# A hybrid decoder layer on eight cores: shift folded into biases, convolution weights built on the core, shuffles in one DMA, and a new order of loads

## The chip, the cores and the metric

The kernel runs on the 8 cores of one Trainium2 chip. Each core computes one batch element, and the cores don't talk to each other. The metric is device time in microseconds (us) of the slowest core. "Granted clock" is the share of full speed that TensorE was given, 1.00 being all of it. The profile views are of the slowest core of one execution; the trace holds all eight. The program lets TensorE write its results into eight banks of 128x512 fp32, in a memory called PSUM, and has VectorE or ScalarE copy ("evict") each result out before it uses the bank again; one such copy took ScalarE 0.60 us in the kernel before (`ev<-ps`, mean of 136).

## The reference, cut to what matters

```python
# x (8, 2048, 1024) fp32, c (8, 1024); one layer
mod = silu(c) @ w_ada + b_ada                       # adaLN: 6 pieces of 1024
sh1, sc1, gt1, sh2, sc2, gt2 = split(mod, 6)
h = rmsnorm(x, g_pre_mix) * (1 + sc1) + sh1
gb, gc, v, a, g = split(h @ w_in, 5)                # 5 x 512 columns
y_short = gb * (causal_dwconv(gc * v, w_short) + b_short)       # 3 taps
u = causal_dwconv(a * sigmoid(g), w_cfm_dw) + b_cfm_dw          # 31 taps
y_cfm = silu(layernorm(u, g_cfm_ln, b_cfm_ln))
y = per_head_rmsnorm(concat(y_short, y_cfm)) * beta_mix
x = x + gt1 * rmsnorm(y @ w_out, g_post_mix)
h = rmsnorm(x, g_pre_ffn) * (1 + sc2) + sh2
x = x + gt2 * rmsnorm(swiglu(h, w_gate_up, w_down), g_post_ffn) # hidden 2816
```

## The kernel before

The kernel brings its own scheduler: the code below is a list of operations with their reads, writes and estimated cost, and the scheduler orders them on each engine. Weights are fp32 in DRAM and bf16 in SBUF; they come by DMAs that POOL issues (the software queue, 53.48 MB in the page), and the other transfers go through SP's hardware queue (48.32 MB). The sequence is cut in four quarters of 512 positions, quarter q holding the positions 4t+q. For the 31-tap convolution the four quarters stand side by side in the partitions, 4 x 32 channels, so that a group of 32 channels takes 9 matmuls. Bringing the projections into that layout, and the result back out of it, is a "shuffle", a DMA from SBUF to SBUF.

The start, with one quarter's gate projections. All four adaLN pieces of the first sub-layer come ahead of the gate weights, and a shuffled tile leaves as four DMAs:

```python
for half in range(2):
    ada_cols(half, "sc", 0, half, (4, 5))
for half in range(2):
    ada_cols(2 + half, "sh", 0, half, (4, 5))
wag = [wload(wag_d[i], 4096, "wag%d" % i) for i in range(2)]
prenorm1(0)
for q in range(4):
    if q < 3:
        prenorm1(q + 1, after=[loads["wada2" if q == 0 else "wag1"]])
    for j in range(4):
        ...                                          # gate and value projections
        act(th, gb.v(), AF.Tanh, scale=0.5, name="tanh")
        dve("scalar_tensor_tensor", ..., name="glu") # (th + 1) * value -> sv
        for c in range(4):
            dv = up.v(g * URow + HALO, g * URow + HALO + CH, 32 * q, 32 * q + 32)
            prs.append((dv.ap, sv.v(p0=32 * c, p1=32 * c + 32)))
        dma("sp", prs, [sv.v()], wv, 0.7, "ushuf")   # four DMAs
```

The convolution (16 groups, weights loaded for two groups at a time), then LayerNorm over channels in one block, then the head norm:

```python
for g in range(NG):
    if g % 2 == 0:
        cw = wload(cw_d[g // 2], 2 * NTAP * 128, "cw%d" % (g // 2))
    ...                                              # 9 matmuls, two evictions, statistics
for g in range(NG):
    dve(ln_sub); dve(ln_mul); act(silu)
for h in range(0, 8, 2):
    ...                                              # head norm, y shuffle: four DMAs a tile
```

Then come the C and v projections, and the output stage: `short(q)` is the 3-tap branch of a quarter, `outproj(q)` its output projection with the residual, and `ada_rows` makes the broadcast row gt1 * g_post_mix, for which it takes a small row from DRAM into one of the two `ys` buffers:

```python
short(0); ada_rows(4, 0, 0, B05); ada_rows(5, 0, 1, B05)
short(1); outproj(0, (2, 4))
short(2); outproj(1, (2, 4))
short(3); outproj(2, (4,)); outproj(3, (4,))
...                                                  # FFN: gate/up, silu, down, residual
```

Four `slot` buffers hold all the weights but `wo` and `wdn`. The two `wo` buffers lie in the memory of `u1`, the convolution's result, so the output projection's weights can only be loaded once the head norm has read it. The four `xc` tiles (x for the residual) lie where the LayerNorm rows were.

Of the kernel before, what the change touches and what calls it, by code (L numbers as in the profile page):

```python
# [36 lines left out]
NV = V_WSH + 12  # L37

# [53 lines left out]
class Prog:  # L92
# [111 lines left out]
    def schedule(self):  # L204
# [53 lines left out]
        while len(seq) < n:  # L258
# [51 lines left out]
            if o.dma is not None:  # L310
                s = max(free[e] + 1000.0, dma_free)
                dma_free = s + o.dma
                o.done = dma_free + 1200.0
            else:
                o.done = free[e] + o.lat
# [149 lines left out]
def build_program():  # L465
# [5 lines left out]
    wag_d = nc.dram_tensor("wag", [2, 128, 4096], F32, kind="ExternalInput").ap()  # L471
    cw_d = nc.dram_tensor("cw", [8, 128, 2 * NTAP * 128], F32, kind="ExternalInput").ap()
# [10 lines left out]
    with es:  # L483
# [35 lines left out]
        assert wdn[1].end <= end_stg  # L519
        xa_s = sb_space("xa", 8, D, F32, at=yT.off)  # L520
        xc_off = cur[0]
        xc_s = sb_space("xc", 4, D, F32)
        lnb = [buf("ln%d" % i, 512, F32, at=xc_off + 2048 * (5 + i)) for i in range(3)]
        xn_s = sb_space("xn", 4, D, BF16)
        ev_s = sb_space("ev", 4, 512, F32)
        ys_s = sb_space("ys", 2, 512, F32)
# [11 lines left out]
        small = buf("small", 192, F32)  # L538
        SM_EPS, SM_EXP, SM_SH, SM_GS, SM_T, SM_SSQ, SM_RS = 0, 1, 2, 18, 34, 50, 114
# [28 lines left out]
        def mm(out, lhsT, rhs, start, stop, n=512, reads=(), name="", **kw):  # L568
            return P.op("pe", lambda e: e.matmul(out.ap, lhsT=lhsT.ap, rhs=rhs.ap, start=start, stop=stop),  # L569
                        reads=[lhsT, rhs] + list(reads), writes=[out], cost=max(n / 2.4 + 2.8, 60.0), lat=280.0,  # L570
                        name=name, **kw)

        def act(out, in_, func, n=512, reads=(), writes=(), name="", bias=None, scale=1.0, accum=None, npt=0, **kw):
# [5 lines left out]
            tb = "silu" if func in (AF.Silu, AF.Tanh) else "exp" if func in (AF.Ln, AF.Exp) else None  # L579
# [14 lines left out]
        def dma(eng, pairs, reads, writes, us, name="", **kw):  # L594
            def fn(e):
                return [e.dma_start(out=val(o_), in_=val(i_)) for o_, i_ in pairs]  # L596
            o = P.op(eng, fn, reads=reads, writes=writes, cost=(1000.0 if eng == "pool" else 70.0) * len(pairs), dma=us * 1000.0,
                     name=name, **kw)
            o.ndma = len(pairs)
            return o  # L600


        loads = {}

        def wload(src, n, name):
            s = Tile(slot_s)
            v = s.v(0, n)
            loads[name] = dma("pool", [(v, src)], [], [v], 128 * n * 4 / 350e3, name=name)
            return s
# [8 lines left out]
        dve("memset", [], [blk32.v()], 250, "c4", ap=blk32.t[:, :], constant=0.0)  # L618
        dve("memset", [], [blk64.v()], 250, "c5", ap=blk64.t[:, :], constant=0.0)

        dve("memset", [], [ones_ln.v()], 250, "c6", ap=ones_ln.t[:, :], constant=0.0)
        for p in range(4):
            a, b = 32 * p, 32 * p + 32
            dve("memset", [], [ones_ln.v(0, 128, a, b)], 180, "c7", ap=ones_ln.t[a:b, a:b], constant=1.0 / 512.0)
            dve("memset", [], [blk32.v(0, 128, a, b)], 180, "c7", ap=blk32.t[a:b, a:b], constant=1.0 / 64.0)
# [12 lines left out]
        act(ct, View(vc(V_C, 8), [K_V]), AF.Silu, n=8, name="csilu")  # L638
# [12 lines left out]
        def ada_cols(piece, kind, l, half, banks):  # L651
# [15 lines left out]
            else:  # L667
                bcol = V_BADA + 16 * l + 8 + 4 * half
                dve("tensor_tensor", [b.v(), K_V], [("sh", l, half)], 80, "ada3", out=sm(SM_SH + c, 4), in0=b.v(0, 4),
                    in1=vc(bcol, 4), op=ALU.add)  # L670

        def ada_rows(piece, l, half, banks):
# [6 lines left out]
            tv = Tile(ys_s).v()  # L679
# [22 lines left out]

        def to_hT(xns, q, l, last, banks):

            for quarter in range(4):
# [9 lines left out]
                for kk in range(2):  # L715
# [4 lines left out]
                    if quarter % 2 == 0:  # L720
# [9 lines left out]
        def prenorm1(q, after=()):  # L730
            xns = []
            last = None
            for b in range(4):
                i = 4 * q + b
                xt = Tile(xa_s).v()
                dma("sp", [(xt, xq[q, b])], [], [xt], 1.5, "xload", after=after)
# [6 lines left out]
        xns = []  # L743
        for half in range(2):
            ada_cols(half, "sc", 0, half, (4, 5))
        for half in range(2):
            ada_cols(2 + half, "sh", 0, half, (4, 5))
        wag = [wload(wag_d[i], 4096, "wag%d" % i) for i in range(2)]
        prenorm1(0)
# [5 lines left out]
        B05 = (0, 1, 2, 3, 4, 5)  # L755
        for q in range(4):
            if q < 3:
                prenorm1(q + 1, after=[loads["wada2" if q == 0 else "wag1"]])
            for j in range(4):
                w, o = wag[j // 2], (j % 2) * 2048  # L760
                gb, ab = bank('mm', *B05), bank('mm', *B05)
                proj(gb, w, o, q, "pg", also=[ab])
                proj(ab, w, o + 1024, q, "pa")
                th = Tile(ev_s).v()
                act(th, gb.v(), AF.Tanh, scale=0.5, name="tanh")
                sv = Tile(stg_s)
                dve("scalar_tensor_tensor", [th, ab.v()], [sv.v()], 750, "glu", out=sv.v(), in0=th, scalar=1.0, in1=ab.v(),
                    op0=ALU.add, op1=ALU.mult)
                prs, wv = [], []
                for c in range(4):  # L770
                    g = 4 * j + c
                    dv = up.v(g * URow + HALO, g * URow + HALO + CH, 32 * q, 32 * q + 32)
                    prs.append((dv.ap, sv.v(p0=32 * c, p1=32 * c + 32)))
                    wv.append(dv)
                dma("sp", prs, [sv.v()], wv, 0.7, "ushuf")
# [5 lines left out]
        for g in range(NG):  # L781
            if g % 2 == 0:
                cw = wload(cw_d[g // 2], 2 * NTAP * 128, "cw%d" % (g // 2))
            b = bank('mm', *B05)
            for s in range(NTAP):
                o = ((g % 2) * NTAP + s) * 128
# [3 lines left out]
            act(uv, b.v(), AF.Identity, reads=[K_V], bias=vc(V_BCF + g), scale=0.5, npt=1, name="cv_ev")  # L790
            s1 = Tile(sq_s).v()
            act(s1, b.v(), AF.Square, reads=[K_V], bias=vc(V_BCF + g), scale=0.5, npt=1, name="cv_sq")
# [12 lines left out]
        P.shift = LN_SHIFT  # L805
        last_silu = None
        for g in range(NG):
# [3 lines left out]
            last_silu = act(uv, uv, AF.Silu, reads=[K_V], bias=vc(V_BLN + g), scale=vc(V_GLN + g), npt=2, name="silu")  # L811
        for h in range(0, 8, 2):
# [8 lines left out]
            rr = Tile(rr_s, line="hdrr")  # L821
            act(rr.v(), st.v(), AF.Ln, n=1024, reads=[("eps",)], bias=sm(SM_EPS), npt=1, name="hd_ln", order=[last_silu])
            act(rr.v(), rr.v(), AF.Exp, n=1024, scale=-0.5, name="hd_exp")
            for h2 in range(2):
                for gg in range(2):
# [6 lines left out]
                    prs, wv = [], []  # L832
                    j, c = g // 4, g % 4
                    for p in range(4):
                        o = (4 + j) * S + p * CH
                        dv = yT.v(o, o + CH, 32 * c, 32 * c + 32)
                        prs.append((dv.ap, sv.v(p0=32 * p, p1=32 * p + 32)))
                        wv.append(dv)
                    dma("sp", prs, [sv.v()], wv, 0.7, "yshuf")
        P.shift = 0.0  # L840
# [6 lines left out]
        dma("sp", [(gtg[0].t[:, :], r_d[0:1, :].to_broadcast([128, D]))], [], [gtg[0].v()], 1.6, "rowb", after=[loads["cw5"]])  # L847
        wcv = [None, None]
        for j in range(4):
            if j % 2 == 0:  # L850
                wcv[j // 2] = wload(wcv_d[j // 2], 4096, "wcv%d" % (j // 2))
            w, o = wcv[j // 2], (j % 2) * 2048
            cb = cvb[j]
            for q in range(4):
# [4 lines left out]
                act(cs, b1.v(), AF.Copy, name="c_ev")  # L859
                ov = cb.v(q * URow + HALO, q * URow + HALO + CH)  # L860
                dve("tensor_tensor", [cs, b2.v()], [ov], 690, "cv", out=ov, in0=cs, in1=b2.v(), op=ALU.mult)
# [7 lines left out]
        wb = wload(wb_d, 4096, "wb")  # L869
        last_exp = [None]  # L870

        def short(q):
            for jp in range(2):
                st = pair('sh', 6)
                yss = [Tile(ys_s), Tile(ys_s)]
                for j2 in range(2):
                    j = 2 * jp + j2
                    b3, b4 = bank('mm', *B05), bank('mm', *B05)
                    proj(b3, wb, j * 1024, q, "pb", also=[b4])
                    bs = Tile(ev_s).v()  # L880
                    act(bs, b3.v(), AF.Copy, name="b_ev")
# [11 lines left out]
                rr = Tile(rr_s)  # L893
                act(rr.v(), st.v(), AF.Ln, n=1024, reads=[("eps",)], bias=sm(SM_EPS), npt=1, name="sh_ln", order=[last_silu])
# [46 lines left out]
        short(2)  # L941
        outproj(1, (2, 4))
        short(3)
# [5 lines left out]
        npc = [0]  # L949
        for half in range(2):  # L950
            for pc in range(11):
                n_ = npc[0]
                npc[0] += 1
                early = half == 0 and pc < EARLY
                w = wload(wgu_d[pc], 4096, "wgu%d" % pc)
                for jj in range(2):
                    j = 2 * pc + jj
                    for s in range(2):
                        q = 2 * half + s
                        gb, ub = (bank('gu', 0, 1, 2, 3), bank('gu', 0, 1, 2, 3)) if early else (bank('gu', *range(8)), bank('gu', *range(8)))  # L960
                        for u, b in enumerate((gb, ub)):
                            for k in range(8):
                                o = ((jj * 2 + u) * 8 + k) * 128
                                mm(b.v(), w.v(o, o + 128), hv(k, q), k == 0, k == 7, name="gu", also=[ub] if u == 0 and k == 0 else ())
                        sl = Tile(ev_s).v()
                        act(sl, gb.v(), AF.Silu, name="fsilu", order=[last_exp[0]])
                        av = actT.v(j * 1024 + s * 512, j * 1024 + s * 512 + 512)
# [115 lines left out]
```

## Time and profile before

| | before |
|---|---|
| time, median of 4 runs | 849.3 us (846.68 to 849.69) |
| profiled span, slowest core | 847.7 us |
| TensorE busy | 749.6 us, 88% |

The first line of the profile's page gives each engine's busy time, its share of the span and its instructions. For the kernel before:

```profile
PE 749.6 (88%) x3737; PEld 349.5 (41%) x3808; DVE 273.6 (32%) x408; ACT 256.1 (30%) x409; POOL 83.0 (10%) x185
```

TensorE (PE) is far above the rest.

### The profile page before, as it was taken

The page shows a single profiled execution, that of the slowest core. Times are in us where ns is not written, and L with a number is a line of the kernel's source. Part 1 is how long each engine was busy: PE and PEld are TensorE (multiplying, and loading weights), DVE is VectorE, ACT ScalarE, POOL GpSimd, SP SyncE. Part 2 cuts the span into 40 slices and gives each one's busy share as a digit, 9 for nine tenths or more (in the row PEclk, how much of TensorE's full clock was granted, in tenths as well). Part 3 has the DMA queues.
Part 4 walks back from the last instruction along what each step waited for, and adds up shares of the span by engine and source line. Part 5 has one row for each costly group of instructions (what it writes and reads, how often), then busy time and mean ns, then how long its engine had stood idle before and what let it go on. Part 6 is the DMA issues. An engine that isn't in the chain of part 4 may idle for free.

```text
span 847.7 us, 10294 instructions; the slowest of 8 cores (834.2 to 847.7 us)
## 1 busy us (share of the span) xinstructions
PE 749.6 (88%) x3737; PEld 349.5 (41%) x3808; DVE 273.6 (32%) x408; ACT 256.1 (30%) x409; POOL 83.0 (10%) x185
## 2 busy tenths in 40 slices
PE   0177999967859798899999999999999999999996
PEld 0134544433324344444444444444444444444442
DVE  3114521482223466645421132122222211111222
ACT  1135525694205466734331111111111111111111
POOL 2103100000000112221200000000100000000100
PEclk9998999979979899999999999999999999999999
DMA  8998149959676334996899676233344544001221
GB/s 153 187 203 243 34 79 160 165 96 198 134 141 124 100 115 110 189 254 163 164 164 198 110 134 114 51 124 115 110 99 68 82 75 76 0 1 49 101 75 75
DMA packets 26066, 102.46 MB, mean 121 GB/s; under 512 B 4256, under 2 KB 8480, under 8 KB 20512
## 3 DMA queue, kind: packets, MB, share of 16 engines
q0 software_dynamic: 7344, 53.48, 38.0%
q1 hardware_dynamic: 18672, 48.32, 18.6%
q8 instruction: 31, 0.51, 0.2%
q14 instruction: 19, 0.16, 0.1%
HBM read 134.29 MB, written 16.78 MB: 178 GB/s over the span
## 4 chain that ended last, share of the span: by engine, by line
PE 74%; DMA 12%; DVE 4%; issue 4%; ACT 3%; SPq 2%; POOL 1%; POOLq 0%; DVEq 0%; ACTq 0%
PE ps L569 72%; DMA yT<-stg 5%; DMA xa<-x 4%; DMA slot<-wada 4%; SPq L596 2%; ACT junk L581 1%; DVE u L585 1%; PE ps L712 1%; ACT rr L581 1%; DVE xc L585 1%; POOL small L589 1%; DVE ps L585 1%; ACT L581 0%; DVE yT L585 0%; DVE ys L585 0%
## 5 line engine op out<-in xcount | busy, mean ns | idle before, releaser
L569 PE MATMUL ps<-hT,slot 128*128 128x512 bf16 x2002 | 460.1, 385 | 23.4 <-DVE small L585 8.7
L569 PEld LDWEIGHTS ps<-hT,slot 128*128 128x128 bf16 x2048 | 201.2, 99 | 267.0 <-issue 37.8
L581 ACT ACTIVATE ev<-ps 128x512 f32<-128x512 f32 x136 | 81.0, 595 | 301.2 <-PE ps L569 292.6
L569 PE MATMUL ps<-wdn,actT 128*128 128x512 bf16 x689 | 151.3, 379 | 0.7
L585 DVE TENSOR_TENSOR actT<-ev,ps 128x512 bf16<-128x512 f32 x88 | 60.4, 686 | 204.1 <-PE ps L569 196.2
L569 PEld LDWEIGHTS ps<-wdn,actT 128*128 128x128 bf16 x704 | 68.9, 98 | 83.0
L585 DVE SCALAR_TENSOR_TENSOR ps<-ps,small,gtg 128x1024 f32<-128x1024 f32 x32 | 41.4, 1293 | 138.2 <-POOL small L589 138.2
L581 ACT ACTIVATE junk<-ps 128x1024 bf16<-128x1024 f32 x32 | 32.7, 1022 | 166.7 <-PE ps L569 158.1
L569 PE MATMUL ps<-wo,yT 128*128 128x512 bf16 x252 | 58.6, 384 | 4.2 <-DVE xc L585 3.6
L589 POOL TENSOR_SCALAR small<-small 128x1 f32<-128x1 f32 x64 | 16.2, 254 | 370.3 <-ACT junk L581 369.7
L712 PE MATMUL ps<-ident,xn 128*128 128x128 bf16 x256 | 21.4, 247 | 28.9 <-DVE xn L585 27.3
L585 DVE TENSOR_TENSOR xc<-ps,xc 128x1024 f32<-128x1024 f32 x32 | 39.1, 1223 | 4.0 <-DVE ps L585 4.0
L569 PEld LDWEIGHTS ps<-wo,yT 128*128 128x128 bf16 x256 | 25.1, 99 | 36.1 <-issue 8.2
L589 POOL TENSOR_TENSOR small<-small 128x1 f32<-128x1 f32 x64 | 37.5, 585 | 9.5 <-POOL small L589 0.6
L569 PE MATMUL ps<-up,slot 128*128 128x512 bf16 x141 | 33.4, 379 | 0.2
L712 PEld LDWEIGHTS ps<-ident,xn 128*128 128x128 bf16 x256 | 19.1, 112 | 33.8 <-issue 32.2
L596 POOL DMA_DIRECT2D slot<-wgu x22 | 12.3, 558 | 198.0 <-PE ps L569 197.8
L581 ACT ACTIVATE hT<-ps,small 128x512 bf16<-128x512 bf16 x32 | 23.2, 775 | 20.7 <-PE ps L712 11.8
L569 PE MATMUL ps<-cact,slot 128*128 128x1 bf16 x256 | 7.9, 165 | 22.1 <-DMA slot<-wada 16.9
L581 ACT ACTIVATE junk<-xa 128x1024 bf16<-128x1024 f32 x16 | 16.8, 1053 | 30.6 <-DMA xa<-x 30.0
L585 DVE SCALAR_TENSOR_TENSOR stg<-ev,ps 128x512 bf16<-128x512 f32 x16 | 11.0, 688 | 37.3 <-PE ps L569 31.3
L585 DVE SCALAR_TENSOR_TENSOR stg<-u,vt,rr 128x512 bf16<-128x512 f32 x16 | 11.7, 750 | 32.6 <-DMA yT<-stg 30.5
(62 smaller groups left out, 328.1 us busy)
## 6 DMA issues: line engine op xcount, KB each, us to landing
slot<-wgu POOLq DMA_DIRECT2D x22, 1024.0 KB, 10.2
slot<-wada POOLq DMA_DIRECT2D x12, 1024.0 KB, 16.6
xa<-x SPq DMA_DIRECT2D x16, 512.0 KB, 12.7
xc<-x SPq DMA_DIRECT2D x16, 512.0 KB, 5.5
x1s<-xc SPq DMA_DIRECT2D x16, 512.0 KB, 6.0
xc<-x1s SPq DMA_DIRECT2D x16, 512.0 KB, 3.9
out<-xc SPq DMA_DIRECT2D x16, 512.0 KB, 2.6
slot<-cw POOLq DMA_DIRECT2D x8, 576.0 KB, 7.9
```

What stands on the lines that cost most here:

```text
L569: return P.op("pe", lambda e: e.matmul(out.ap, lhsT=lhsT.ap, rhs=rhs.ap, start=start, stop=stop), reads=[lhsT, rhs] + list(reads), writes= ...
L581: return P.op("act", lambda e: e.activation(out=out.ap, in_=in_.ap, **a), reads=[in_] + list(reads), writes=[out] + list(writes), cost=c, ...
L585: return P.op("dve", lambda e: getattr(e, meth)(**{k: val(v) for k, v in kw.items()}), reads=reads, writes=writes, cost=cost, lat=80.0, na ...
L589: return P.op("pool", lambda e: getattr(e, meth)(*a, **kw), reads=reads, writes=writes, cost=cost, lat=80.0, name=name)
L596: return [e.dma_start(out=val(o_), in_=val(i_)) for o_, i_ in pairs]
L712: P.op("pe", lambda e, ov=ov, iv=iv: e.transpose(out=ov.ap, in_=iv.ap, identity=ident.t[:, :]), reads=[iv, ident.v()], writes=[ov], cost=6 ...
```

## The change

The intent is to start TensorE sooner, to take bytes out of the DMA queues where they hold it up, and to take small work out of its way. There are five parts.

1. The adaLN shift is not added to h but becomes biases after the projections (`w.T @ shift`, one-column matmuls). Two of the four adaLN pieces are enough for the first projection. Quarter 0's projections wait raw in SBUF for their biases. The first loads of x move from SP's queue into POOL's, in line with the weights, and the gate weights come in four loads with buffers of their own.
2. Convolution weights are multiplied out of a small table (0.29 MB in DRAM) on VectorE, instead of eight loads of 1.18 MB.
3. A new channel layout makes each shuffled tile one DMA and not four.
4. LayerNorm and head norm are spread behind the C/v projections; the weights of this stage wait for the last input shuffle (HELD); the first four residual x loads go behind the last y shuffle.
5. In the output stage: `short(3)` ahead of `outproj(1)`, more banks, four `ys` buffers, one own buffer for the row, and gate/up products of quarter 0 first.

```diff
-        for half in range(2):
-            ada_cols(2 + half, "sh", 0, half, (4, 5))
-        wag = [wload(wag_d[i], 4096, "wag%d" % i) for i in range(2)]
-        prenorm1(0)
+        wag = [wload(wag_d[i], 2048, "wag%d" % i, wag_s) for i in range(4)]
+        xts.append(xload(1))
+        prenorm1(0, xts[0])
 ...
+                if q == 0:
+                    act(rg, gb.v(), AF.Copy, name="raw")
+                    dve("tensor_copy", [ab.v()], [ra], 690, "raw", out=ra, in_=ab.v())
+                    raws.append((j, q, rg, ra))
 ...
+                    ada_cols(2 + half, "sh", 0, half, (6, 7))
+                bias([(wag[i // 2], (i % 2) * 1024) for i in range(8)], (6, 7), 0)
 ...
-                cw = wload(cw_d[g // 2], 2 * NTAP * 128, "cw%d" % (g // 2))
+            dve("tensor_tensor", [wv.v(), dlt.v()], [cw.v()], 1300, "cwm", out=ov,
+                in0=dlt.t[:, :].unsqueeze(1).unsqueeze(3).to_broadcast([128, NTAP, 32, NPH]),
+                in1=w3.unsqueeze(2).to_broadcast([128, NTAP, 32, NPH]), op=ALU.mult)
 ...
-                    dma("sp", prs, [sv.v()], wv, 0.7, "yshuf")
+                    ysl.append(dma("sp", [(dv, sv.v())], [sv.v()], [View(None, wk)], SHUF, "yshuf"))
+        behind = {i: [lambda g=g: ln(g) for g in range(2 * i, 2 * i + 2)] for i in range(8)}
+        for i in range(4):
+            behind[8 + 2 * i] = [lambda h=h: head_norm(h) for h in (2 * i,)]
 ...
-        ys_s = sb_space("ys", 2, 512, F32)
+        row_s = sb_space("row", 1, 512, F32)
+        ys_s = sb_space("ys", 4, 512, F32, at=u1.off)
 ...
-            tv = Tile(ys_s).v()
+            tv = Tile(row_s).v()
 ...
         short(2)
+        short(3)
         outproj(1, (2, 4))
-        short(3)
 ...
+        ys = [o for o in P.q["sp"] if o.name == 'yshuf'][-1]
+        xs = [o for o in P.q["sp"] if o.name == 'xload2'][:4]
 ...
+                L.remove(o)
+            i = L.index(ys) + 1
 ...
+            L[i:i] = xs
```

## The prediction

> **What bounds the kernel now.** I read the page first: TensorE is busy 88% of the span, so it is the bound, and a gain can only come from its idle or slowly clocked time. The second view, busy time by stretch cut where TensorE changes its task, says where that time lies (columns: stretch, its length, busy time and count of each engine, granted clock, DMA share, GB/s).
>
> ```profile
> 0.00:50.78 50.78, 7.24 (x160) 7.21 (x162) 11.32 (x52) 8.98 (x14) 8.84 (x22) 1.00 0.95 175
> 50.78:71.54 20.76, 15.92 (x62) 6.63 (x63) 5.70 (x8) 6.64 (x12) 3.51 (x8) 0.94 1.01 238
> 71.54:120.52 48.98, 48.54 (x284) 25.45 (x290) 19.09 (x31) 24.16 (x40) 8.81 (x17) 0.96 0.35 92
> 120.52:158.12 37.60, 37.39 (x171) 17.03 (x174) 7.70 (x20) 19.16 (x31) 4.23 (x8) 1.00 0.89 153
> 158.12:253.66 95.54, 70.31 (x397) 31.79 (x402) 42.61 (x73) 44.26 (x64) 4.22 (x8) 0.86 0.79 146
> 253.66:356.36 102.70, 89.50 (x429) 40.87 (x436) 57.11 (x70) 60.56 (x92) 17.30 (x39) 0.95 0.53 125
> 356.36:839.69 483.33, 480.69 (x2239) 220.56 (x2283) 127.59 (x154) 91.20 (x157) 35.29 (x81) 1.00 0.48 106
> 839.69:847.70 8.01, 0.00 (x0) 0.00 (x0) 2.52 (x2) 1.11 (x2) 0.79 (x2) 0.75 0.16 65
> ```
>
> The stretches are: loading before the first projection; gate projections (two rows); the 31-tap convolution; the C/v projections with LayerNorm and head norm behind them; the short branch and output projection; the FFN; the tail. The FFN and the convolution are full. Idle: 43.5 us at the start, 5.3 in the gate projections, 25.2 in the C/v stage, 13.2 in the output stage, 8.0 in the tail.
>
> The chain that ended last names what the idle parts wait for (start, duration, what):
>
> ```profile
> 3.15 31.52 DMA slot<-wada
> ...
> 36.56 31.65 DMA xa<-x
> ...
> 174.66 1.35 DVE u L585 x3
> ...
> 189.91 14.49 DMA yT<-stg
> ...
> 209.86 11.58 DMA yT<-stg
> ...
> 229.55 13.20 DMA yT<-stg
> ```
>
> So: weights and x at the start; then, in the C/v stage, the LayerNorm run on VectorE (32 operations, 161.4 to 182.6 us, with evictions of projections queued behind them: the first three come at 182.48), then three shuffles. The waits of that stage, TensorE's own and VectorE's on the shuffle (total us, times, longest):
>
> ```profile
> DVE stg L585 <- DMA yT<-stg: 30.5, 5, 12.0
> ...
> PE ps L569 <- DVE small L585: 8.7, 1, 8.7
> PE ps L569 <- ACT sq L581: 7.7, 4, 5.0
> PE ps L569 <- DVE cvb L585: 7.4, 3, 4.0
> PE ps L569 <- ACT ev L581: 1.2, 2, 1.0
> ```
>
> VectorE stands on a staging buffer that a shuffle has not emptied, so it evicts no projection, and TensorE runs out of PSUM banks.
>
> [...] in the FFN the chain repeats every 10.79 us for 50 matmuls (49 recorded, some records are missing), and 14 matmuls after a stall took 4.91 us[...]. [...] a shuffle piece lands in 1.8 us on idle DMAs and in 8 to 14.7 us while the software queue streams weights. [...] by 83.25 us some 23.4 MB of fp32 source had landed, 289 GB/s counted from 2.3 us. [...]
>
> **Start and gate projections.** Before, x (four tiles, 2.1 MB), four adaLN pieces (8.4 MB fp32) and the first gate weights (2.1 MB) precede the first projection at 50.78 us. The change folds the shift into biases applied after the projections, so only two adaLN pieces are needed first, and cuts the gate weights into 1 MB loads. What must land falls from 12.6 to 2.1 + 4.2 + 1.05 = 7.3 MB. At 289 GB/s that is 25 us plus 2.3; the slower rate of the first 42 us (10.5 MB in 40 us, 262 GB/s) gives 30. First projection: about 30, 20 earlier. That gain does not last whole. The next tiles queue behind in one software queue: gate weights, x of quarter 1 (12.6 MB landed at 46 us), the two shift pieces (61), x of quarters 2 and 3 (69, 76). In the new order of instructions TensorE stands in line for both shift pieces inside quarter 1, then computes biases, and the first quarter's raw gates hold staging buffers until then. Following the order: quarter 1 starts near 51, its last projections near 75 (they need banks that the late gates release), quarter 2 near 80, and two quarters of 13.8 us with transposes of 2 put the convolution at 107 to 110; at 310 GB/s it would be 103. I take 107 for 120.5: **-13.5 us**.
>
> **Convolution.** The eight weight loads (1.18 MB each) go; VectorE builds the diagonal weights from a small table. 16 operations of 1152 elements[...]; four are made ahead. [...] Hidden: **0**.
>
> **C/v stage.** LayerNorm is now spread two groups behind each of the first eight projections, one head norm behind every second of the last eight; each staged tile leaves in one DMA instead of four (64 issues of 0.59 us become 16); x for the residual no longer queues ahead of the shuffles; weights for this stage are loaded during the convolution. Work: 272 matmuls x 0.216 = 58.8, 128 one-column ones in 4.0 (32 took 0.99 us), 64 new bias columns 2.0: 64.8 us against 95.5 taken. What remains lost: in the first half VectorE has 32 x 0.60 us (28 LayerNorm operations took 16.95 us back to back in the timeline) and 8 x 0.75, 25 us beside 29.6 of TensorE, so only the latency of the statistics shows (5 us from the last convolution to the first subtraction with its scale, less what spare banks cover): 3 us. In the second half three 2.1 MB weights still stream when the first four tiles shuffle, and four staging buffers remain, so one or two waits of 8 us stand, partly covered by spare banks: 6 us. Stage 74: **-21.5 us**.
>
> **Output stage.** Short branch 3 before output projection 1, more banks and buffers for it, and gate/up products of quarter 0 first, so they can fill holes without quarter 1. Idle is 13.2 us, slow clock (5% of 89.5) about 4. VectorE and ScalarE stay half busy, and their chains (evict, square, ln, exp, multiply) remain: I take off 8. **-8 us**.
>
> **Sum.** The 160 bias columns (5 us) are counted in the stages. 849.3 - 13.5 - 21.5 - 8 = 806.3; the size of the C/v gain leans to the low side, since the held loads look placed against just that wait, so I say **805 us**.
>
> **Rivals.** (1) The start's gain is given back: DMA share is 1.01 until about 83 us, and x of quarter 3 cannot land before 76, so the convolution starts at 115 and the total is 815 to 820. For it: the two in-order waits on shift pieces. Against: 2.1 MB less must land by then, and nothing waits for convolution weights. (2) The shuffles stay the wait of the C/v stage: same bytes, same staging buffers, weights still streaming; the stage keeps 20 lost us and the total is 820 to 825. For it: the 8 to 14 us landings above. Against: the residual's x, which stood ahead in the same queue for the first of the three waits, is gone. (3) VectorE becomes the bound in the convolution[...]; 813. (4) The stages close fully: C/v dense, output stage dense, 785 to 790.
>
> **Range and chances.** Start gain 5 to 18, C/v 10 to 28, output 2 to 13, not moving together: 788 to 825. Slower would need gains to vanish in three independent places. Faster by over 2% (below 832) 0.95, same 0.045, slower 0.005.
>
> **What would show it.** First wide matmul near 30 us; convolution weights' first use at 103 to 110; its stretch still 38 us with VectorE about 30 busy; C/v stage 70 to 80 us with clock above 0.93; VectorE's wait on the shuffle well under 30.5; FFN and tail unchanged. Wrong if the convolution starts after 115, if the C/v stage is over 85, or if the FFN gets a wait.

Three figures given there without a source can be found in the trace of the kernel before: 0.216 us a matmul is the FFN's 10.79 us for 50; 0.75 us is what VectorE took for 512 columns of `ys<-ps,vt,ev` (750 ns, median); and 310 GB/s is near what the text's own numbers give for the time after 42 us (23.4 less 10.5 MB in 41.25 us, 313 GB/s). The DMA share that rival 1 puts at 1.01 until about 83 us is 1.01 from 50.78 to 71.54 us and 0.81 from there to 83.25.

## The result, and the profile after

The changed kernel takes 818.56 us, median of 10 runs (fast ones 816.45 to 819.71), against 849.01 for the kernel before, median of 16 in the same rounds. Executions in which one die ran at a lower clock are left out of the means. The ratio of the fast runs is 0.9641, with a 95% interval of 0.9629 to 0.9653: faster by over 2%. (Ratios here divide the mean time of one kernel's fast runs by that of the other's of the same rounds, so they are not quite the ratio of the medians quoted.) The profiled span went from 847.7 to 818.2 us.

The page's first line of the changed kernel: VectorE has 24.5 us more work (the built weights are 21.5 of it), and TensorE's busy time hardly moved, so the gain is idle time of TensorE.

```profile
PE 752.8 (92%) x3969; PEld 351.1 (43%) x3969; DVE 298.1 (36%) x429; ACT 261.2 (32%) x413; POOL 92.6 (11%) x196
```

Busy time by stretch of the changed kernel, cut at the same changes of task as before (the same columns: stretch, length, PE, PEld, DVE, ACT, POOL, granted clock, DMA share, GB/s):

```profile
0.00:29.96 29.96, 5.81 (x97) 5.26 (x98) 11.23 (x47) 8.62 (x14) 16.17 (x35) 1.00 0.93 180
29.96:54.93 24.97, 18.06 (x81) 8.33 (x81) 5.78 (x8) 7.59 (x14) 6.31 (x12) 0.93 1.01 212
54.93:113.21 58.28, 52.57 (x400) 27.48 (x401) 26.74 (x42) 25.98 (x43) 10.04 (x16) 0.94 0.44 121
113.21:151.62 38.41, 38.41 (x207) 17.82 (x206) 23.26 (x33) 19.96 (x32) 2.22 (x4) 1.00 0.69 113
151.62:226.96 75.34, 67.89 (x481) 32.77 (x478) 44.10 (x75) 45.30 (x63) 3.69 (x7) 0.95 0.58 102
226.96:320.00 93.04, 82.11 (x387) 36.48 (x386) 47.12 (x61) 55.32 (x80) 13.14 (x29) 0.96 0.72 168
320.00:810.80 490.80, 487.99 (x2328) 222.97 (x2326) 137.36 (x163) 97.96 (x169) 40.26 (x92) 1.00 0.47 106
810.80:818.20 7.40, 0.00 (x0) 0.00 (x0) 2.52 (x2) 0.48 (x2) 0.79 (x2) 0.63 0.18 71
```

| step | before | after | moved by | forecast |
|---|---|---|---|---|
| first wide matmul | 50.78 | 29.96 | -20.8 | about 30 |
| convolution starts | 120.52 | 113.21 | -7.3 | -13.5 |
| convolution | 37.60 | 38.41 | +0.8 | 0 |
| C/v stage | 95.54 | 75.34 | -20.2 | -21.5 |
| output stage and FFN together | 586.03 | 583.84 | -2.2 | -8 |
| tail | 8.01 | 7.40 | -0.6 | 0 |

The output stage and the FFN have to be read together, because the number of gate/up steps that run ahead went from six to four, and with it the line between the two. The rows below the first make 29.5 us, the difference of the two spans.

The chain that ended last (start, duration, what) goes, as before, through x at the start and through shuffles; a row of 256 KB is new in it:

```profile
20.02 49.70 DMA xa<-x
...
193.25 18.97 DMA yT<-stg
...
214.60 17.50 PE ps L581 x99
...
237.65 0.69 DVE gtg L597
...
238.50 0.70 DVE gtg L597
239.26 25.27 DMA row<-rows
```

And the waits (total us, times, longest), TensorE's first, then VectorE's on transfers:

```profile
PE ps L746 <- DVE xn L597: 24.6, 3, 14.8
PE ps L581 <- DVE small L597: 7.4, 1, 7.4
PE ps L581 <- DVE ys L597: 6.2, 1, 6.2
```

```profile
DVE stg L597 <- DMA yT<-stg: 15.5, 3, 8.4
...
DVE gtg L597 <- DMA row<-rows: 4.7, 2, 4.4
```

The first line of the waits is the start (14.8 us until the first x is normalised) and two later tiles of x. The second is the C/v stage: its whole idle time is this one wait at 214 us, and behind it stands the shuffle issued at 193.25, which needed 19 us. (`small` is only the tiny operation that VectorE did last; VectorE had been standing on the staging buffer.) The third is new: at 267.6 us TensorE waits 6.2 us for the short branch's `ys`, and the chain shows why. The second row load was issued at 239.26 us, the moment VectorE had used the first row, and took 25 us to land.

These are the waits of core 7, the slowest. In the same execution the C/v wait is 5.2 to 7.4 us on four cores (spans 813.5 to 818.2 us) and at most 1.9 us on the other four (806.1 to 809.3 us): it takes the slow cores, and the metric is the slowest one. The wait for `ys` is on all eight cores, 1.1 to 9.6 us.

### The profile page after: what moved, and what is told of

Same layout as the page of the kernel before. It is cut to its first block, busy times and chain, and to the rows that moved or that the text cites. A ratio compares the mean times of both kernels' runs of the same rounds, so it can differ in the third digit from the quotient of the medians.

```text
span 818.2 us, 10617 instructions; the slowest of 8 cores (806.1 to 818.2 us)
## 1 busy us (share of the span) xinstructions
PE 752.8 (92%) x3969; PEld 351.1 (43%) x3969; DVE 298.1 (36%) x429; ACT 261.2 (32%) x413; POOL 92.6 (11%) x196
## 4 chain that ended last, share of the span: by engine, by line
PE 74%; DMA 15%; DVE 3%; ACT 3%; issue 2%; POOL 1%; POOLq 0%; DVEq 0%; ACTq 0%; SPq 0%
PE ps L581 73%; DMA xa<-x 7%; DMA row<-rows 3%; DMA yT<-stg 2%; DMA slot<-wgu 2%; ACT junk L593 2%; PE ps L746 1%; DVE xc L597 1%; DVE ps L597 1%; POOL small L601 1%; DMA up<-stg 1%; ACT ev L593 0%; DVE stg L597 0%; ACT rs L593 0%; POOL xa L608 0%
## 5 line engine op out<-in xcount | busy, mean ns | idle before, releaser
L581 PE MATMUL ps<-hT,slot 128*128 128x512 bf16 x1792 | 398.8, 381 | 16.0 <-DVE small L597 7.4
L581 PEld LDWEIGHTS ps<-hT,slot 128*128 128x128 bf16 x1792 | 174.9, 98 | 228.0 <-issue 22.5
L593 ACT ACTIVATE ev<-ps 128x512 f32<-128x512 f32 x88 | 52.4, 597 | 217.0 <-PE ps L581 217.0
L581 PE MATMUL ps<-hT,wag 128*128 128x512 bf16 x256 | 61.8, 401 | 2.7 <-DMA wag<-wag 2.0
L601 POOL TENSOR_SCALAR small<-small 128x1 f32<-128x1 f32 x64 | 18.0, 282 | 358.8 <-ACT junk L593 358.3
L593 ACT ACTIVATE ev<-ps,small 128x512 f32<-128x512 f32 x44 | 29.8, 680 | 39.0 <-PE ps L581 35.1
L581 PEld LDWEIGHTS ps<-hT,wag 128*128 128x128 bf16 x256 | 25.5, 102 | 33.9 <-issue 8.6
L581 PE MATMUL ps<-up,cw 128*128 128x512 bf16 x144 | 33.6, 379 | 0.0
L597 DVE TENSOR_TENSOR cw<-dlt,wv 128x1152 bf16<-128x1152 bf16 x16 | 21.5, 1357 | 9.9 <-PE ps L581 7.7
```

The source lines that it names most:

```text
L581: return P.op("pe", lambda e: e.matmul(out.ap, lhsT=lhsT.ap, rhs=rhs.ap, start=start, stop=stop), reads=[lhsT, rhs] + list(reads), writes= ...
L593: return P.op("act", lambda e: e.activation(out=out.ap, in_=in_.ap, **a), reads=[in_] + list(reads), writes=[out] + list(writes), cost=c, ...
L597: return P.op("dve", lambda e: getattr(e, meth)(**{k: val(v) for k, v in kw.items()}), reads=reads, writes=writes, cost=cost, lat=80.0, na ...
L601: return P.op("pool", lambda e: getattr(e, meth)(*a, **kw), reads=reads, writes=writes, cost=cost, lat=80.0, name=name)
```

## The experiments

Twelve kernels ran, four at a time on one chip, each beside the kernel before. Where not said otherwise an edit is made to the changed kernel. On the chip of the first four, the kernel before was unsteady (849.17 to 863.82 us, median 860.55), so I read those four against the changed kernel's 818.56 us, or the 820.18 of the later control, and do not use their ratios. The unedited changed kernel did not run on that chip; on the two chips where it did, it differs by 1.6 us.

### The first four: take out one part at a time

**LayerNorm and head norm in one block again** (`ln_block`):

```diff
-        behind = {i: [lambda g=g: ln(g) ...] for i in range(8)}
-        for i in range(4):
-            behind[8 + 2 * i] = [lambda h=h: head_norm(h) for h in (2 * i,)]
+        behind = {}
+        for g in range(NG):
+            ln(g)
+        for h in range(0, 8, 2):
+            head_norm(h)
```

> The changed kernel with one part undone: all LayerNorm and head norm work stands in one block before the C/v projections again. Theory (the block on VectorE was the larger cause of the 20 us that the C/v stage gained): TensorE idles again behind it, the stage grows from 75.3 us by 10 to 15, the total goes from 818.6 to 828 to 834. Rival (the shuffles were the cause, the spread is incidental): the stage grows by under 4, total at most 822. A third way: the shuffles start some 10 us earlier this way and meet fewer weight loads, so part of the loss is paid back and the total is 822 to 828.

It took 817.25 us (816.24 to 818.06): not slower. My theory of this part fell. TensorE's waits show what was exchanged:

```profile
PE ps L581 <- ACT sq L593: 5.7, 3, 4.0
...
PE ps L581 <- DVE cvb L597: 3.1, 2, 2.3
```

The block costs several short waits, the longest 4.0 us. In return the 7.4 and the 6.2 us are gone: the y shuffles are issued from 179 us on rather than 192, the residual x at 214 rather than 227 and lands by 245 rather than 262. In this kernel, spreading the norms delays what comes after them by about as much as it saves.

**Each shuffle as four DMAs again** (`shuf4`), in the new layout, so a piece covers 8 destination partitions by 4 rows:

```diff
-            ush.append(dma("sp", [(dv, sv.v())], ...
+            ush.append(dma("sp", [(dv[8 * c:8 * c + 8], sv.v(p0=32 * c, p1=32 * c + 32)) for c in range(4)], ...
```

(and the same for the y shuffles)

> The changed kernel with every shuffle issued as four DMAs of 32 rows again, same bytes and same layout. Theory (the number of issues was not what cost; the rows wait behind the weight loads in the DMA engines): within 2 us of 818.6. Rival (the queue's 64 issues of 0.59 us were the wait): the C/v stage grows by 5 to 10 us, total 824 to 829.

829.68 us (828.83 to 831.22), 9.5 to 11 slower: my theory fell. But these pieces are cut differently from those of the kernel before, which left open whether the count or the cut costs. `shuf4b` below settles it.

**The residual x not moved** (`xres_early`): the block that moves the four loads is deleted.

> The changed kernel without the step that moves the first four residual x loads behind the last head shuffle; they are issued before the shuffles, during the convolution. Theory (moving them shifted a wait from one stage to another, and they would have landed long before the shuffles start): the C/v stage unchanged within 2 us, the output stage loses most of the 6.2 us stall near 262 to 267 us, since x and the row behind it no longer land at 259 to 265; total 812 to 818. Rival (they stand in front of the shuffles as in the kernel before): C/v stage longer by 5 or more, total 820 to 824.

825.94 us, the median of the three fast runs (825.42 to 829.49), 6 to 7 slower; here too my theory fell, and the rival held, a little beyond its range. TensorE's and VectorE's waits:

```profile
PE ps L581 <- DVE small L597: 27.4, 2, 16.2
```

```profile
DVE stg L597 <- DMA yT<-stg: 35.9, 3, 24.5
```

The `xc` buffers come free only at 180 us, so the loads are issued just ahead of the shuffles. The first four shuffles then take 27 us each.

**The shift pieces ahead of the gate weights** (`shift_first`), to take the early start away and leave the rest:

```diff
+        for half in range(2):
+            ada_cols(2 + half, "sh", 0, half, (4, 5))
         wag = [wload(wag_d[i], 2048, "wag%d" % i, wag_s) for i in range(4)]
```

(and the later call is removed)

> The changed kernel with the two shift pieces loaded before the gate weights, as in the kernel before; biases are still applied after the projections. Theory (the convolution's start is set by when x of quarters 2 and 3 has landed, and the same bytes must land by then in both orders): the first wide matmul comes at about 44 us instead of 30, the convolution starts at 110 to 117 instead of 113.2, total 816 to 822. Rival (the early start is worth its 14 us): convolution at 125, total 829 to 833.

822.54 us (822.15 to 823.0), 2 to 4 slower: the theory's direction, just outside of its ranges. The first wide matmul comes at 44.24 us, 14.3 later, the convolution at 119.39, only 6.2 later, and the end 2 to 4 later. That is the early start's exchange rate: less than half of it reaches the convolution, and under a third the end. The edit undoes 14.3 of the 20.8 us; the rest, with x in POOL's queue and smaller gate loads, was not taken apart.

### The second four: what is left, and the control

**Control** (`after_ctl`), the changed kernel unedited:

> Control: the changed kernel itself once more, so that the variants of this batch have their parent on the same chip. 816 to 820 us if this chip is like the one of the first measurement.

820.18 us (816.99 to 824.78), ratio 0.9658 (0.962 to 0.9696). Slightly more spread than in the first measurement.

**adaLN columns 6 to 9 ahead of the C/v projections** (`ada_early`). In the changed kernel the four weight slots were full from 148 to 167 us and the DMAs idle (share 0.01); the last weights then streamed beside the shuffles.

```diff
-            if j == 0:
-                ada_cols(6, "sc", 1, 0, B05)
-            elif j == 1:
-                ada_cols(7, ...); ada_cols(8, ...)
-            elif j == 2:
-                ada_cols(9, "sh", 1, 1, B05)
+            # in front of the first C/v projection, after wcv0 is asked for:
+            ada_cols(6, ...); ada_cols(7, ...); ada_cols(8, ...); ada_cols(9, ...)
```

> adaLN columns 6 to 9 are computed before the C/v projections instead of inside them, so the four weight slots come free some 25 us earlier and the last 2.1 MB weights stream in the hole of the DMA between 148 and 167 us and not beside the y shuffles. Theory (the y shuffles are slow because weights stream beside them): shuffles land in 3 to 8 us instead of 18 to 19, the 7.45 us wait of TensorE at 214 us falls below 3, time 5 to 8 us less, 810 to 814. Rival (the shuffles are slow by their own issue and count): they stay at 15 us or more, the wait stays, time 817 to 820. Third way: wada6 to 9 land late enough that TensorE waits for them in front of the C/v projections: slower by up to 5 us.

816.12 us, the median of the three fast runs (815.33 to 818.62), ratio 0.9613 (0.9588 to 0.9638): 0.45% of 849 us, some 3.8 us, less than the control. The two intervals overlap, so the gain in time is not clear of the scatter, and it falls short of the 5 to 8 us of the theory; what the edit did to the waits is clear. DMA issues of the page (what, queue, operation, count, size, median us from issue to landing), first of the changed kernel, then of this one:

```profile
yT<-stg SPq DMA_DIRECT2D x16, 128.0 KB, 8.8
```

```profile
yT<-stg SPq DMA_DIRECT2D x16, 128.0 KB, 3.4
```

The first twelve shuffles now land in 2.9 to 3.4 us (2.9 to 3.7 over all eight cores), and the 7.4 us wait is gone (at most 0.3 us on any core): the shuffles were slow because weights streamed beside them. The last four are not better off, 10 to 27 us, because the weights of the output projection and of the FFN stream from 213 us on. TensorE now waits there, 3.2 us for a shuffle and 5.7 us (at 263.5 us) for VectorE's residual adds. VectorE itself waits for no staging buffer any more, but for the row:

```profile
DVE gtg L597 <- DMA row<-rows: 13.6, 1, 13.6
```

The row lands at 258.6 us, and the second one, in the same buffer, at 262.8. So what took the place of the removed wait is the subject of the next run.

**A second row buffer** (`row2`):

```diff
-        row_s = sb_space("row", 1, 512, F32)
+        row_s = sb_space("row", 2, 512, F32)
```

> A second buffer for the broadcast row of the quarter, so that the second row load need not wait until VectorE has used the first. Theory (the new 6.2 us wait of TensorE at 267.6 us hangs on the single row buffer, through which the issues that follow stand in line): the wait falls to under 2 us, time 3 to 6 us less. Rival (the loads land late, 259 to 264 us, because 2.1 MB weights for the output stage stream ahead of them on all engines): the wait stays at 5 to 6 us, time unchanged within 1.5 us.

814.21 us (813.09 to 816.31), ratio 0.9587 (0.9565 to 0.9609): 0.71%, some 6 us, less than the control, from one digit. The two rows are issued together (237.4 and 238.9 us) and land at 262.9 and 263.6. In the control the second is issued at 265.9 and lands at 269.3. TensorE's waits, first of the control, then of this run:

```profile
PE ps L581 <- DVE ys L597: 4.2, 1, 4.2
```

```profile
PE ps L581 <- DVE small L597: 6.7, 1, 6.7
PE ps L581 <- DMA yT<-stg: 5.0, 1, 5.0
```

The wait for `ys` is gone, here and on the other seven cores (in the control it is on all eight, 1.1 to 7.2 us), and quarter 1's output projection starts at 266.13 us and not at 270.62. A part of it moved: TensorE now waits 5.0 us for the last shuffle at 255 us. The time shows the gain clearly (the intervals do not overlap), and the profiles of the slowest cores account for 4.5 us of it.

**Convolution weights loaded again** (`cw_loaded`):

```diff
-            dve("tensor_tensor", [wv.v(), dlt.v()], [cw.v()], 1300, "cwm", ...
+            dma("pool", [(cw.v(), cw_d[g])], [], [cw.v()], 1.85, "cw")
```

> The convolution weights are loaded again (16 loads of 0.59 MB in the software queue, the same bytes as before the change) instead of being built on VectorE from the small table. My theory (building is hidden behind TensorE, and what it buys is room in the queue): VectorE's 21.5 us go, the convolution stretch stays 38 to 39 us, but the held weights and the quarters' x come later: 0 to 6 us more. Rival (the loads were hidden before as well, the build buys nothing): same within 1.5 us. Second rival (the build was costing): 2 us or more less.

884.61 us, ratio 1.042: far outside of what either theory allowed, and the edit is to blame. The four held weights (2.1 MB each) are issued at 123.7 to 126 us in the middle of the convolution loads, in the same queue. The convolution's next weights, issued from 126 us on, land at 158 and later (26.3 us from issue to landing, the median of the 16 loads). TensorE's order of instructions meanwhile put the adaLN columns into the convolution's hole and waited for each of them:

```profile
PE ps L582 <- DMA slot<-wada: 24.4, 6, 6.7
```

As a test of the part this run says nothing. `cw_loaded2` repeats it.

### The third four: settle the attributions, and a better version

**Convolution weights loaded, held weights behind the last of them** (`cw_loaded2`): the edit above, and

```diff
-  after=ush[15:16] if name in HELD ...
+  after=cwl[15:16] if name in HELD ...      # cwl: the convolution loads
```

> Convolution weights loaded again in 16 DMAs, and the held weights of the next stage now stand behind the last of them, so that no convolution load waits behind a 2.1 MB weight as in the first attempt. My theory (the build buys the room of 9.4 MB in the queue during the convolution, when the next stage's weights must come): the convolution is unchanged at 38 to 40 us, the C/v projections start late, TensorE waits there for wcv and adaLN weights, 5 to 20 us slower than the changed kernel. Rival (hidden anyway): within 2 us.

834.47 us (832.51 to 836.08), ratio 0.9832 (0.9798 to 0.9865): about 15 us slower than the changed kernel. The convolution starts at 117.69 us, 4.5 later (its first loads lie ahead of quarter 3's x), and is all but full. Then TensorE waits for the first weight of the next stage (from TensorE's timeline: start, length, and in brackets the idle time before it and what ended it):

```profile
163.32 0.99 PE L582 MATMUL ps<-shb,slot 128*128 128x1 bf16 x32 [5.30 <-DMA slot<-wcv]
```

The C/v stage starts at 163.3 us instead of 151.6. So the built weights are worth up to some 15 us, not through VectorE or TensorE but through 9.4 MB that the queue does not carry. It is an upper bound, as holding the next weights behind the very last load was my choice.

**Only the y shuffles in four DMAs, in pieces of 32 destination partitions as before the change** (`shuf4b`):

```diff
-  ysl.append(dma("sp", [(dv, sv.v())], ...
+  ysl.append(dma("sp", [(dv[:, p], sv.v().ap[p:128:4]) for p in range(4)], ...
```

> Only the y shuffles in four DMAs each again, cut as before the change in pieces of 32 destination partitions (the earlier test cut both shuffles, in pieces of 8 destination partitions by 4 rows). Theory, taken from that earlier test (the number of issues on one queue is what costs, 0.67 us each and 2.7 us a tile): again 8 to 12 us slower than the changed kernel, ratio 0.974 to 0.980. Rival (the cut in 8 partitions [...] that was the cost): within 2.5 us of the changed kernel, ratio 0.962 to 0.968.

831.04 us, the median of the three fast runs (829.19 to 831.7), ratio 0.9788 (0.9751 to 0.9824): 11 to 12.5 us slower than the changed kernel, so it is the count. VectorE's wait on the shuffles and TensorE's wait that comes of it:

```profile
DVE stg L597 <- DMA yT<-stg: 34.6, 7, 11.3
```

```profile
PE ps L581 <- DVE small L597: 24.8, 2, 16.5
```

One issue keeps SP for 0.5 to 0.6 us (median 0.59 for the 64 of the kernel before, 0.55 for the 16 of the changed kernel), so among the first four tiles one of four DMAs comes every 2.5 to 2.7 us and one of a single DMA every 0.66. The transfers themselves are not slower: the first four tiles have landed by 213.7 us here and by 212.5 in the changed kernel. But SP works on the 16 tiles until 249 us, and in the changed kernel it is through with them at 227. So the later tiles run into the weights of the output stage, though every piece is a quarter of the size.

**The kernel before, with only the residual x moved** (`before_xlate`): the block from the end of the diff of the change, put into the kernel before.

> The kernel before with one part of the change alone: the first four residual x loads moved behind the last y shuffle. Theory (the part is worth what taking it out of the changed kernel cost, some 9 us): 838 to 842 us, the first four shuffles land in 8 us or less instead of 14.5, VectorE's wait on the shuffle falls from 30.5 to under 22. Rival (four pieces a shuffle and the weights keep the shuffles slow, so the part is worth little by itself): 845 to 850 us.

845.81 us (845.65 to 848.61), ratio 0.9977 (0.9938 to 1.0016): the same. The rival's number held, but its reason only in part: the move does what it should, and the time does not follow. VectorE's waits on transfers, and TensorE's longest in that part of the kernel:

```profile
DVE stg L585 <- DMA yT<-stg: 20.5, 5, 10.1
...
DVE gtg L585 <- DMA ys<-rows: 17.0, 1, 17.0
```

```profile
PE ps L569 <- ACT sq L581: 14.7, 3, 12.2
```

The wait on the shuffles falls from 30.5 to 20.5 us, and the four DMAs of the first tile land in 6.2 to 6.8 us instead of 14.4 to 14.7. But the residual and the row, now behind, run into the weights of the output stage (x lands at 263 to 278 us), and TensorE waits 12.2 us at 281.7 us. TensorE's waits of 0.15 us and more in the C/v stage fall by 8 us, and those of the output stage rise from 13 to 21: what one stage won the next one paid.

**Four moves together** (`combo`): `ada_early`, `row2`, the broadcast row of the first half (0.5 MB, needed in the output stage) loaded after the last input shuffle instead of beside quarter 1's x, and

```diff
-        ys = [o for o in P.q["sp"] if o.name == 'yshuf'][-1]
+        ys = [o for o in P.q["sp"] if o.name == 'yshuf'][7]
```

> Changed kernel plus four moves of loads and small work: adaLN columns 6 to 9 before the C/v projections, a second row buffer, the broadcast row of the first half loaded after the convolution's last input shuffle, and the first four residual x loads issued after the eighth y shuffle and not after the last. Theory (what is left in the C/v and output stages is transfers that stand behind streaming weights, and each of these takes one out of the way): the residual x lands before 225 us instead of 259 to 262, first wait of TensorE in the output stage under 3 us, time 6 to 12 us below the changed kernel, ratio to the kernel before 0.950 to 0.957, 807 to 813 us. Rival (the waits only move, since the same bytes have to come before the output projection): ratio 0.960 to 0.966, 815 to 820 us. x of quarter 1 should land some 2 us earlier, and the convolution should start 1 to 3 us earlier.

811.51 us (807.46 to 815.32), ratio 0.9561 (0.9516 to 0.9607): 7 to 9 us below the changed kernel, and the fastest of all, though its interval overlaps that of `row2` alone (0.9565 to 0.9609), so that by the metric the other three moves are not shown to add anything. The mean span of the eight cores, which scatters less, says that they do: 801.5 us over the fast runs (800.1 to 802.0 from run to run) against 806.4 (805.1 to 806.9) for `row2`, with the kernel before at 841.3 and 841.8 on the two chips. The slowest core, which has the long wait below, hides it. x of quarter 1 landed at 46.2 us instead of 48.9, and the convolution started at 110.53. The residual lands by 215 us, and the waits of the output stage fall to parts of a microsecond. But one wait on the slowest core is longer than the 7.4 us of the changed kernel (core 4 has one of 8.0 us there, the other six cores none):

```profile
228.70 3.57 PE L581 MATMUL ps<-hT,slot 128*128 128x512 bf16 x8 [10.37 <-DVE small L597]
```

The residual's 2.1 MB are issued at 202 us, and the third four shuffles, issued from 207 on, land beside them and beside the first output weights, in 8 to 18 us. TensorE's waits of 1.2 us and more in total, added up, are 47.2 us in this profile and 54.7 in the changed kernel's, a difference near the gain; the rival, waits that only move, was half right.

## Why the prediction was right or wrong

The time, 818.56 us, lies inside the range of 788 to 825, and faster by over 2% was right. The central 805 was 13.6 us too low. By its own steps:

- **Start.** The first wide matmul was put at about 30 us and came at 29.96; the shift pieces (61) and x of quarters 2 and 3 (69 and 76) landed at 61.4, 69.7 and 78.3; quarter 2 (80) started at 81.4. The term that was mis-sized is the last: "two quarters of 13.8 us with transposes of 2 put the convolution at 107 to 110". 80 + 2 x 13.8 + 2 is already 109.6, so the 107 that I took did not follow from its own terms. The stretch from 81.4 to the convolution took 31.8 us, 2.2 more than these terms: the granted clock of its first half was 0.89 (the view of stretches, cut more finely, below), and 64 matmuls there needed 15.66 us and not 13.8. Together 2.6 (my own sum), 1.4 (quarter 2) and 2.2 make the 6.2 us by which the gain was 7.3 and not 13.5. The convolution's weights are first used at 113.21 us, outside of the 103 to 110 that the prediction named as its sign. The first rival (gain given back, convolution at 115, total 815 to 820) came closest to the outcome, and `shift_first` confirms its direction; that its total holds the outcome is in part luck, since 5.8 of the 13.6 us were lost in the output stage, of which it says nothing.

```profile
81.40:97.50 16.10, 16.10 (x79) 7.26 (x77) 6.61 (x12) 4.40 (x8) 2.28 (x4) 0.89 0.15 50
```

- **Convolution.** VectorE hides behind TensorE, as predicted: a stretch of 38.41 us, full. VectorE was busy there for 23.3 us, not the "about 30" of the prediction's signs, since four of the sixteen builds ran ahead. The arithmetic behind the 0 is cut, since no trace before the change showed what a built weight takes. The trace after it does: 1.36 us (columns: instructions, then busy us and mean ns), which with the 0.43 us of the cast is 1.79 us a group, where TensorE takes 2.40 (38.41 / 16):

```profile
L597 DVE TENSOR_TENSOR cw<-dlt,wv 128x1152 bf16<-128x1152 bf16 x16 | 21.5, 1357 | 9.9 <-PE ps L581 7.7
```

  But "Hidden: 0" only asked what the build costs. What it is worth was counted nowhere by itself: with the weights loaded, the next stage starts 11.7 us later and the end comes some 15 us later (`cw_loaded2`, an upper bound).

- **C/v stage.** 74 us forecast, 75.34 measured, clock 0.95: right in size, in part by luck: 7.5 us of idle time where 9 were left in, and 67.9 us of work where 64.8 were counted. The explanation was wrong in one of its parts. I wrote first of the LayerNorm spread behind the projections. `ln_block` shows that this is worth nothing within the runs' scatter: it moves the shuffles later by what it saves. One DMA a tile, which I named only in passing and then, after the trace, took for unimportant, is worth 11 to 12.5 us (`shuf4b`), and the moved residual 6 to 7 (`xres_early`). Their sum is near the stage's 20 us, but that is no proof, since they don't add: the residual moved in the kernel before, where each tile still is four DMAs, gains nothing (`before_xlate`). That what remained, "one or two waits of 8 us", is due to weights streaming beside the first four tiles was right: there was one, of 7.4, and `ada_early` removes it by removing the weights.

- **Output stage.** "I take off 8" had no measured ground, and 2.2 came. The idle time went from 13.2 to 10.9 us (with the line to the FFN moved), and 6.2 of that was new. The cause is a line of the change that I read past: the row came out of the two `ys` buffers into an own space with one buffer. `row2` gives back about 6 us; that 2.2 + 6 is close to the 8 does not give the 8 a ground.

- **FFN and tail.** Unchanged, as predicted, but for one wait of 1.2 us for a gate/up weight, at 464 us.

Still open: what holding the weights (HELD) does by itself, what the new order of the short branch and of gate/up does, what x in POOL's queue does, and how the 16 us of the VectorE wait on shuffles divide among weights, residual and each other. The control and the changed kernel differ by 1.6 us between chips, so differences under 3 us between single variants are not claimed, and those near it (`shift_first`, `ada_early`) rest on their traces.

## What to carry to other kernels

Moving one transfer alone did not cure the idle engine here (`before_xlate`, ratio 0.9977): ask which bytes will stand beside it in its new place, and check the next stage's waits before counting the gain. Here small transfers that release buffers did best as few issues (64 instead of 16 on one queue cost 11 to 12.5 us, `shuf4b`), and away from megabytes of weights whose place could be elsewhere (a 128 KB shuffle landed in 2.9 to 3.4 us without them and in 10 to 27 us beside them, `ada_early`, its first twelve and last four): try both. Read every buffer count that a change touches, since one buffer fewer in a space that looked unimportant cost about 6 us here, most of what was expected of the stage. And look at all the cores: a wait that decides the slowest may be missing on half of them.
